# Ordering a two-layer hybrid backbone's instructions by another simulated clock

## The chip, the cores and the metric

The kernel runs on one core of a Trainium2 chip. The metric is the device time of one execution in microseconds (us); lower is better. The names of the engines are short throughout: PE is TensorE's matmul, PEld its weight load, DVE is VectorE, ACT is ScalarE, POOL is GpSimd, SP is SyncE, whose queue issues every DMA of this kernel (SPq in the profile).

## The reference

The input is 1024 latent tokens and 256 context tokens, 1024 wide, in float32, batch 1. Two layers follow, each with a modulated RMSNorm, one input projection, two branches side by side, one output projection, a gate and a residual:

- layer 0: an RWKV-7 recurrence over 8 heads of 64, in both directions, beside a Mamba-2 state-space pass over 16 heads of 64 with state 128, in chunks of 128 tokens, in both directions;
- layer 1: an mLSTM with 4 heads of 256, in chunks of 128, in both directions, beside grouped-query attention of 16 query heads on 4 key heads of 64 with a two-axis rotary embedding, over latent and context keys.

In short form:

```python
for l in range(2):
    h  = rmsnorm(x, g[l]) * (1 + scale) + shift          # the same for ctx
    y  = (rwkv || mamba)(h @ ab_w_in) if l == 0 else (mlstm || attention)(h @ cd_w_in)
    x  = x + gate * (y @ w_out)                           # ctx too, after layer 0
out = rmsnorm(x, norm_final)
```

The recurrences of the latent tokens start from the states that the context tokens left.

## The kernel before

Everything is written in one program of a tile framework: Python functions write instructions for named engines on named tiles, and when the context closes a scheduler orders them. The scheduler runs a simulation of the core: whenever an engine (or a DMA queue) is free on the simulated clock, it is given the earliest written instruction for it whose operands are there and whose buffer is free on that clock. The result is one fixed queue for each engine, which the chip runs strictly in order; waits between engines are semaphores. Each `pool.tile(..., tag=..., bufs=n)` is one of n buffers under a tag, so a load into a tag waits until an older tile of that tag has had its last reader. All loads and stores (`load`, line 179, and `store`, line 182) go through SP's one queue. All plain matmuls are recorded by line 212 and all transposes by line 215, so they are told apart by the tiles they write.

The written order is itself interleaved by hand: generators stand for streams of work, and `lockstep`, `pace` and `mix(a, b, r)` take steps of one and of another in a set ratio. The stages, in order:

1. The modulation vectors of layer 0 (`ada_mod`), and the normed input (`norm_in`), kept on chip as a high and a low part (`hh`, `hl`).
2. `l0_gemm`: the projections of layer 0, one block of 128 columns at a time. `wsplit` loads a weight block `wr`, ACT copies its high part `wh` (line 358), POOL subtracts to get the low part `wl` (line 359); PE adds three products (`hh` by `wh`, `hl` by `wh`, `hh` by `wl`) into PSUM tiles tagged `mm`. Results go to DRAM.
3. `mamba_bwd` beside the gate projections, then `mamba_fwd` beside the RWKV projections. For each chunk and group (20 steps) the forward pass loads a 1 MB broadcast tile `R` (one buffer), DVE adds to it (lines 1083 and 1084) and takes a minimum into `E` (line 1086), ACT exponentiates, POOL makes `sel` out of eight small instructions (line 1073), DVE multiplies `E` by `sel` (line 1097) and by `cb` (line 1098), PE multiplies `E` into PSUM tiles `mb`; lines 1139, 1140, 1151 and 1153 scale and add up the output, which is normed (lines 1158 to 1163) and transposed in the next step. For this stage alone PE's queue is kept as written: `with s.tc.manual_schedule(engines={mybir.EngineType.PE})`.
4. The RWKV stage: `out_part` (the Mamba half of the output projection, tiles `oa`) beside two streams in lockstep, each with two of the four pairs of heads. A stream is 20 units per pair: `rwkv_prep` (which has the square root of line 628 and the reciprocal of line 629), `rwkv_unit` (which makes the products `KB`, lines 718 and 719, and inverts a triangular matrix by doubling, tiles `rec`, `Tm`, `Xs`, `TT`) and `rwkv_chain` (the recurrence proper, tiles `ch`).
5. `out_gemm`: the rest of layer 0's output projection, and layer 1's norm.
6. `l1_gemm`: layer 1's projections beside the mLSTM, backward and forward.
7. `out_part` again, for the mLSTM half, beside the attention's keys (`attn_keys`: load `akx`, norm and rotate, split into `akk`, transpose into `tp`).
8. `attention`: scores, softmax, transposes and values, three heads deep.
9. `out_gemm` for the last half (weights loaded into `owr`, four buffers; activations into `oyr`, cast to `oyh`) and the final norm.

The scheduler's clock is chosen where the context is opened, in `kernel`:

## Time and profile before

| what | us |
|---|---|
| median of 3 runs | 3853.24 |
| lowest and highest | 3848.49, 3854.36 |
| the profiled execution | 3854.14 |
| its span, from the first to the last instruction | 3852.0 |
| PE busy in it | 3472.1 |
| DVE busy | 2324.0 |
| ACT busy | 1575.6 |
| POOL busy | 1059.2 |

The profile is one execution. An engine's busy time counts its own work and not the waits; matmuls are pipelined and their ends are modelled, so that a busy PE may still not be at its peak. Idle time of an engine is put down to the instruction whose semaphore came last. The granted clock is the share of TensorE's full speed that it had.

### The profile page before, as it was taken

What the parts mean: (1) busy time and instruction counts of PE and PEld (TensorE: products, weight loads), DVE (VectorE), ACT (ScalarE), POOL (GpSimd) and SP (SyncE); (2) the same over time, 40 slices, a digit from 0 to 9 for tenths busy, and PEclk for the clock granted to TensorE, in tenths of its full rate; (3) what the DMA queues carried; (4) which work ended last, traced back from release to release, by engine and by line L of the source; (5) the groups of instructions that cost most, each with busy time, mean ns of one, the idle gap of its engine ahead of it and who ended that gap; (6) DMA issues with size and microseconds to landing.
All of it is one profiled execution on the core that took longest, in us unless ns stands there. A gap on an engine that the chain in (4) does not pass through costs nothing.

```text
span 3852.0 us, 74955 instructions
## 1 busy us (share of the span) xinstructions
PE 3472.1 (90%) x29178; PEld 2714.9 (70%) x29178; DVE 2324.0 (60%) x4501; ACT 1575.6 (41%) x3675; POOL 1059.2 (27%) x1029
## 2 busy tenths in 40 slices
PE   7999998886898898799678999999999779999978
PEld 3687876664577777688567897788888556666547
DVE  3576487773566766667567507433343687877655
ACT  3232233333435656556433313222222226666641
POOL 0112266553322121211103112112212353333330
PEclk9999998896799988799789999999999889999999
DMA  6526454435433222211132323644543540100023
GB/s 233 178 74 196 136 176 153 158 116 177 146 120 99 66 69 68 80 50 45 47 130 82 126 82 115 199 153 148 163 156 116 184 133 17 28 22 17 15 77 112
DMA packets 394282, 429.68 MB, mean 112 GB/s; under 512 B 81376, under 2 KB 317760, under 8 KB 391368
## 3 DMA queue, kind: packets, MB, share of 16 engines
q1 hardware_dynamic: 393928, 424.90, 35.0%
q8 instruction: 230, 3.77, 0.4%
q14 instruction: 124, 1.02, 0.1%
HBM read 306.69 MB, written 118.05 MB: 110 GB/s over the span
## 4 chain that ended last, share of the span: by engine, by line
PE 48%; DVE 12%; issue 6%; DMA 6%; ACT 3%; POOL 3%; SPq 2%; ACTq 0%; DVEq 0%; POOLq 0%
PE mm L212 20%; PE rec L212 7%; PE pv L212 5%; PE tp L215 4%; PE sc L212 4%; PE lm L212 2%; PE oa L212 2%; PE ch L212 2%; SPq L179 2%; DMA lRW<-lrow 1%; DVE KB L718 1%; POOL wl L359 1%; DMA lkt<-xo 1%; DMA y<-yt 1%; DVE KB L719 1%
## 5 line engine op out<-in xcount | busy, mean ns | idle before, releaser
L212 PE MATMUL mm<-hh,wh 128*128 128x512 f32 (+1 forms) x1640 | 635.0, 387 | 0.0
L212 PE MATMUL mm<-hh,wl 128*128 128x512 f32 (+1 forms) x1640 | 610.8, 372 | 0.9 <-POOL wl L359 0.9
L212 PE MATMUL mm<-hl,wh 128*128 128x512 f32 (+1 forms) x1640 | 611.3, 373 | 0.0
L359 POOL TENSOR_TENSOR wl<-wr,wh 128x1024 fp32r<-128x1024 f32 x99 | 249.4, 2523 | 544.1 <-ACT wh L358 497.6
L212 PEld LDWEIGHTS mm<-hh,wh 128*128 128x128 f32 x1640 | 315.7, 192 | 67.8 <-issue 12.7
L212 PEld LDWEIGHTS mm<-hl,wh 128*128 128x128 f32 x1640 | 314.9, 192 | 61.4 <-issue 10.6
L212 PEld LDWEIGHTS mm<-hh,wl 128*128 128x128 f32 x1640 | 314.5, 192 | 59.4 <-issue 3.4
L1766 DVE TENSOR_REDUCE amx<-sc 128x1 f32<-128x512 f32 (+1 forms) x384 | 227.9, 596 | 85.3 <-PE sc L212 83.4
L1781 POOL TENSOR_SCALAR aP<-aP,adn,one 128x1280 f32<-128x1280 f32 x128 | 180.3, 1409 | 338.9 <-PE tp L215 116.0
L212 PE MATMUL sc<-akT,aqs 128*128 128x512 f32 (+1 forms) x768 | 247.1, 406 | 8.8 <-ACT aP L1772 8.5
L1772 ACT ACTIVATE aP<-sc,amx 128x512 f32<-128x512 f32 (+1 forms) x384 | 232.5, 618 | 40.8 <-DVE amx L1770 40.1
L212 PE MATMUL pv<-aPT,aV 128*64 128x256 f32 x1280 | 225.5, 398 | 0.5 <-DVE aG L1804 0.5
L215 PE MATMUL tp<-mk,aP 128*128 128x128 f32 x1280 | 216.2, 282 | 0.8 <-POOL aP L1781 0.8
L212 PE MATMUL mm<-wh,hh 128*128 128x256 f32 x736 | 216.4, 294 | 0.0
L212 PE MATMUL mm<-wl,hh 128*128 128x256 f32 x736 | 208.3, 283 | 3.5 <-POOL wl L359 2.6
L212 PE MATMUL mm<-wh,hl 128*128 128x256 f32 x736 | 207.8, 282 | 0.0
L215 PEld LDWEIGHTS tp<-mk,aP 128*128 128x128 f32 x1280 | 148.5, 141 | 83.2 <-issue 41.6
L1787 ACT COPY aPT<-tp 128x512 f32<-128x512 f32 (+1 forms) x256 | 121.5, 482 | 165.8 <-PE tp L215 161.3
L358 ACT CAST wh<-wr 128x1024 fp32r<-128x1024 f32 x99 | 103.2, 1045 | 150.2 <-PE mm L212 119.9
L779 ACT COPY TT<-rec 64x256 f32<-64x256 f32 x400 | 146.4, 366 | 37.8 <-PE rec L212 19.8
L212 PEld LDWEIGHTS sc<-akT,aqs 128*128 128x128 f32 x768 | 119.8, 193 | 50.9 <-ACT aP L1772 39.6
L212 PE MATMUL rec<-Tm,MT 128*64 128x64 f32 x3200 | 138.7, 230 | 13.3 <-DVE Tm L763 6.0
(417 smaller groups left out, 8035.9 us busy)
## 6 DMA issues: line engine op xcount, KB each, us to landing
wr<-in_wcd SPq DMA_DIRECT2D x60, 512.0 KB, 5.5
adaw<-in_ada SPq DMA_DIRECT2D x48, 512.0 KB, 5.2
R<-rowd SPq DMA_DIRECT2D x20, 1024.0 KB, 5.3
wr<-in_wab SPq DMA_DIRECT2D x38, 512.0 KB, 4.1
yr<-y SPq DMA_DIRECT2D x36, 512.0 KB, 4.1
xt<-xtok SPq DMA_DIRECT2D x20, 512.0 KB, 4.9
SV<-vtd SPq DMA_DIRECT2D x320, 32.0 KB, 2.1
lva<-lv SPq DMA_DIRECT2D x19, 514.0 KB, 4.3
```

The lines of the kernel that those rows point to most:

```text
L179: return s.nc.sync.dma_start(out, in_)
L212: return s.nc.tensor.matmul(out, lhsT, rhs, start=start, stop=stop)
L215: return s.nc.tensor.transpose(out, in_, ident)
L358: nc.scalar.copy(hi, raw)
L359: nc.gpsimd.tensor_sub(lo, raw, hi.bitcast(F32))
L718: nc.vector.tensor_mul(KB[H[h], :, h], P[H[h]], a[H[h]])
L719: nc.vector.tensor_mul(KB[H[h], :, 1 - h], P[H[h]], kd[H[h]])
L779: nc.scalar.copy(TT[H[h], :, H[h]], pt[H[h]])
L1766: nc.vector.tensor_reduce(mx[:, i:i + 1], ps[:, :n], AX.X, ALU.max)
L1772: nc.scalar.activation(P[:, k0:k0 + n], pss[i][:, :n], AF.Exp, bias=mx[:, 3:4], scale=0.125, accum_out=dn[:, i:i + 1])
L1781: nc.gpsimd.tensor_scalar(P, P, dn, s.one, ALU.mult, ALU.mult)
L1787: (nc.vector.tensor_copy if s0 == 0 else nc.scalar.copy)(o, pp[:, :n])
```

## The change

One argument where the context is opened. It replaces the machine that the scheduler's simulation runs on, a default model of the core, by a second one, a timeline simulation, with prices and queues of its own. The written program, its tiles, its buffers, the hand-written interleaving and the hand-kept queue of PE in stage 3 are the same.

```diff
--- before.py
+++ after.py
@@ -2021,7 +2021,7 @@
         arrays["in_" + name] = a
         aps[name] = nc.dram_tensor("in_" + name, a.shape, F32, kind="ExternalInput").ap()
     out = nc.dram_tensor("out_0", (T, D), F32, kind="ExternalOutput").ap()
-    with tile.TileContext(nc) as tc:
+    with tile.TileContext(nc, schedule_with_timeline_sim=True) as tc:
         program(nc, tc, aps, out)
     r = run_bass_kernel_spmd(nc, [arrays], core_ids=[0])
     return np.asarray(r.results[0]["out_0"]).reshape(1, T, D)
```

## The prediction

> **What bounds the kernel now.** I read three views in this order: the busy shares, the busy time by stage, and the waits of TensorE (PE) within the stages that are not full.
>
> ```profile
> span 3852.0 us, 74955 instructions
> PE 3472.1 (90%) x29178; PEld 2714.9 (70%) x29178; DVE 2324.0 (60%) x4501; ACT 1575.6 (41%) x3675; POOL 1059.2 (27%) x1029
> ```
>
> PE is busy for 90% of the span. 3852.0 - 3472.1 = 379.9 us are left in which it is not, and only there, and in the lower clock that follows a pause, can another order of the same instructions act. The stretches below are cut at the stages of the program; columns are the stretch, its length, busy us (and count) of each engine, granted clock, DMA share and GB/s.
>
> ```profile
> 100.00:500.00 400.00, 390.88 (x2005) 302.23 (x2004) 239.43 (x243) 118.29 (x191) 94.09 (x111) 1.00 0.47 151
> 500.00:860.00 360.00, 318.06 (x1531) 250.42 (x1530) 282.44 (x360) 120.35 (x181) 218.34 (x218) 0.91 0.44 147
> 860.00:1110.00 250.00, 197.49 (x1252) 131.68 (x1251) 120.76 (x192) 102.85 (x189) 75.91 (x81) 0.77 0.52 156
> 1110.00:1900.00 790.00, 698.03 (x14004) 593.40 (x14002) 535.27 (x1205) 456.67 (x1289) 158.13 (x190) 0.91 0.24 67
> 1900.00:2020.00 120.00, 80.93 (x360) 61.42 (x357) 68.96 (x135) 41.80 (x77) 5.44 (x14) 0.78 0.37 123
> 2020.00:3005.00 985.00, 944.96 (x5381) 825.78 (x5380) 423.73 (x692) 279.24 (x564) 207.40 (x163) 0.98 0.42 133
> 3005.00:3160.00 155.00, 114.34 (x493) 90.20 (x491) 124.51 (x269) 37.84 (x55) 76.25 (x83) 0.85 0.56 176
> 3160.00:3727.00 567.00, 557.45 (x3390) 345.99 (x3390) 429.99 (x1178) 359.02 (x1033) 207.26 (x155) 0.99 0.08 22
> 3727.00:3852.00 125.00, 94.38 (x424) 76.22 (x424) 61.37 (x141) 22.85 (x29) 7.81 (x3) 0.89 0.41 137
> ```
>
> Three stages, the first layer's projections (100 to 500), the second layer's projections with the mLSTM (2020 to 3005) and the attention (3160 to 3727), together 1952 us, run PE at 96 to 98% and the clock at 0.98 to 1.00: no order can give much there, though a bad one can take. The open places are the Mamba forward pass beside the RWKV projections (500 to 860: 41.9 us without PE), the start of the RWKV stage (860 to 1110: 52.5), the RWKV recurrence (1110 to 1900: 92.0), and the joints at 1900, 3005 and 3727 (39.1, 40.7 and 30.6).
>
> **The change part by part.** No instruction, tile or buffer is added or taken away. The scheduler walks a simulated clock; an engine that is free on that clock is given the earliest written instruction whose operands and buffers are ready on it. Only the clock is another. So two instructions that are ready at the same time on either clock keep the written order, and a pair changes places only where the two clocks disagree on which was ready first. PE itself cannot change between the last projections and the end of the Mamba pass, because that part fixes PE's order by hand; there the change acts through VectorE (DVE), ScalarE (ACT), GpSimd (POOL) and the DMA queue of SyncE (SP). The cost of the edit in instructions is 0 us; what follows prices the reordering place by place, against the profiled execution's 3854.14 us (its span is 3852.0; the median of the runs is 3853.24, 0.9 us less, so no correction is needed).
>
> Place 1, the Mamba pass. One stall shows what a wrong clock costs. The columns are start, length, engine, instruction, and in brackets the idle time before it.
>
> ```profile
> 587.07 9.75 POOL L1073 TENSOR_SCALAR sel<-mk,mdfd,mdt 128x128 f32<-128x128 f32 x8
> 596.79 2.82 POOL L359 TENSOR_TENSOR wl<-wr,wh 128x1024 fp32r<-128x1024 f32 x1
> 593.47 1.21 DVE L1086 TENSOR_TENSOR E<-R 128x1024 f32<-128x1024 f32 x1
> 599.64 0.33 SPq L179 DMA_DIRECT2D wr<-in_wab  x1
> 602.07 0.40 SPq L179 DMA_DIRECT2D R<-rowd  x1
> 609.88 1.23 DVE L1083 TENSOR_TENSOR R<-R,mAE 128x1024 f32<-128x1024 f32 x1 [9.18 <-DMA R<-rowd]
> 611.02 0.68 DVE L1139 TENSOR_TENSOR y<-mb,mex 128x512 f32<-128x512 f32 x1
> 611.76 1.12 PE L215 MATMUL mb<-mk,yo 128*128 128x128 f32 x4 [11.51 <-DVE y L1139]
> ```
>
> The buffer R is free at 594.7 (593.47 + 1.21), but its load is issued at 602.07, because the weight load ahead of it in SP's queue waits until POOL's split ends at 599.61 (596.79 + 2.82), and POOL came to that split late, behind eight sel instructions of 9.75 us. Then DVE holds the written-earlier L1139 behind L1083, which waits for R, and PE loses 11.51 us. Both placements say that the present clock believed POOL and this load to be earlier than they were. A clock that prices them nearer to the truth would put R ahead of the weight load, 602.07 - 594.7 = 7.4 us sooner, and L1139 ahead of L1083. PE's waits of the stage that DVE ends:
>
> ```profile
> PE mb L215 <- DVE y L1139: 16.2, 5, 11.5
> PE mb L212 <- DVE yt L1107: 4.7, 2, 2.7
> PE mb L212 <- DVE ss L1159: 4.3, 2, 2.5
> PE mb L212 <- DVE y L1139: 3.9, 2, 3.6
> ```
>
> They add to 29.1 us. Bounds: all of it (-29) if the new clock is right throughout, +42 (the stage's present idle time once more) if it is wrong elsewhere. I take half of the first, -15, since POOL's lateness is partly of a kind that no fixed price holds.
>
> That kind shows in one row: the usual time of L1097 is 1.2 us and the longest 3.4.
>
> ```profile
> L1097 DVE TENSOR_TENSOR E<-E,sel x20: 1211/1222/3419, 341.6 to 828.2; 128x1024 f32<-128x1024 f32 x20
> ```
>
> The long one starts at 597.28, 0.5 us after POOL's split, and ends at 600.70, 1.1 us after that split ends: about its own usual length behind it. The Trainium skill's page "SBUF — State Buffer", section "Summary: rules for kernel authors", says that a DVE instruction with two SBUF inputs and a GpSimd instruction that reads SBUF exclude each other, the second waiting until the first is done; the row agrees with that. By it the end of such a pair depends on which of them comes first by a fraction of a us, and a planned order keeps only part of its worth; without it the same sum would take the whole 29 us. My halving rests on the row alone.
>
> Place 2, the joint before the last projection.
>
> ```profile
> 3727.34 6.29 SPq L182 DMA_DIRECT2D y<-aG  x4
> 3734.86 8.99 SPq L179 DMA_DIRECT2D owr<-in_wcdo  x5
> 3744.38 0.42 SPq L179 DMA_DIRECT2D oyr<-y  x1
> 3752.43 1.22 PE L212 MATMUL mm<-oh,oyh 128*128 128x512 f32 x2 [20.52 <-ACT oyh L1239]
> ```
>
> PE waits 20.52 us. The load of the activations, oyr, stands behind five weight loads of which the fifth waits for one of four buffers; the stores it needs are issued by 3733.6. Issued after the fourth weight load it would be up to 8 us sooner. But the weights that it meets are also on the way, and it depends on those stores, whose landing the clock may place late again. Bounds -8 and 0; I take -4.
>
> Place 3, the joint before the attention.
>
> ```profile
> 3007.76 5.23 SPq L179 DMA_DIRECT2D aV<-av  x10
> 3013.03 0.43 SPq L179 DMA_DIRECT2D akx<-ak  x1
> 3025.05 1.97 PE L215 MATMUL tp<-mk,akk 128*128 128x128 f32 x8 [19.55 <-ACT akk L1724]
> ```
>
> Ten loads of V, needed only in the attention proper, stand ahead of the keys, and PE waits 19.55 us. All eleven are ready at once and are written in this order, so by the rule above either clock leaves them. 0, bounds -5 (the ten go behind) and +5.
>
> Place 4, the recurrence. It is a chain of short steps, and its largest wait of PE is for KB:
>
> ```profile
> PE rec L212 <- DVE KB L719: 17.1, 16, 3.1
> 1307.40 0.42 DVE L718 TENSOR_TENSOR KB<-P,a 64x256 f32<-64x256 f32 x1
> 1307.85 1.75 DVE L629 RECIPROCAL al<-al 128x256 f32<-128x256 f32 x1
> 1309.63 0.42 DVE L719 TENSOR_TENSOR KB<-P,kd 64x256 f32<-64x256 f32 x1
> 1310.11 2.07 PE L212 MATMUL rec<-AR,KB 64*128 64x128 f32 x8 [0.33 <-DVE KB L719]
> L629 DVE RECIPROCAL al<-al x20: 1732/1753/1755, 890.8 to 1545.6; 128x256 f32<-128x256 f32 x20
> ```
>
> A reciprocal of the preparation, 1.75 us, sits between the two KB products of a unit. There are 20 of them: moved to better gaps they give at most 20 x 1.75 = 35 us, and as much is lost if later-written work is let in at 20 more such places. Both ends are open and nothing in the trace leans to one of them: 0, bounds -35 and +35. The start of the stage (860 to 1110) and the joint at 1900 I leave at 0 too: the first lacks weights that are loaded only when the Mamba pass releases its space, the second is a serial finish.
>
> Sum: -15 - 4 + 0 + 0 = -19; 3854.14 - 19 = 3835 us.
>
> **The rivals.**
>
> Slower: the recurrence takes in too much. On the new clock a chain step counts as not yet ready at a moment where on the chip it is, and the free engine starts a longer, later-written piece. For it speaks that this happens already (the reciprocal above) and that the stage is the longest that is not full. Against it: most PE waits there are short. Place: 1110 to 1900. Price: one reciprocal's length in each of 40 pairs of units (80 units, two streams side by side; 790 us / 40 = 19.8 us a pair) is 40 x 1.75 = 70; half of the pairs, 35. With the 19 still won elsewhere the time is 3854 + 35 - 19 = 3870, and without it 3889; with every pair hit, 3924. It decides from 19 / 40 = 0.5 us a pair on.
>
> Slower by table loads: the order on ACT can place more changes between functions.
>
> ```profile
> L628 ACT ACT_TABLE_LOAD x20 | 25.7, 1283 | 0.4
> 591.74 1.28 ACT L1160 ACT_TABLE_LOAD   x1
> 593.03 0.20 ACT L1160 ACTIVATE ss<-ss 128x1 f32<-128x1 f32 x1
> ```
>
> All 20 square roots of the preparation have a load already, so there is little room for more; 20 more on the chain would be 20 x 1.283 = 26 us, less the 19: 3861. The Trainium skill's page "ScalarE: Activation LUTs", section "What ACT_TABLE_LOAD costs", counts a further drain of about 1.38 us to each switch; here the function starts 1.29 us after its load does, so the trace does not show it. By the page the same 20 would cost about 53 us, as an estimate.
>
> No change: where the clocks agree the queues stay, the stall at 599 does too, and the time is 3854 give or take 0.2%; the program being left wholly as it was is part of this case. For it speaks that PE's waits are short nearly everywhere, so the present clock cannot be far off.
>
> **How the numbers follow.** Forecast 0.48; slower by the recurrence 0.28; by table loads 0.08; no change 0.16. 0.2% (7.7 us) is about what a measurement of this kernel can tell from no change. The forecast's own range is 3800 (the whole 29 in place 1, 8 in place 2 and half of place 4's 35: -54) to 3846. Whole range 3785 (a little beyond, since several stages can gain at once) to 3910 (between the slower case at half and at every pair). Faster 0.48, same 0.16, slower 0.36.
>
> **What would show it.** Right: in the stretch 500 to 860 POOL's and DVE's order changed, R's load ahead of the weight load, the wait of DVE's L1083 for R (9.18 us here) gone and PE's 41.9 us without work down to about 27. At the last joint oyr is issued before the fifth weight load and 20.52 is down by about 4. The ten loads of V still lead the keys. The full stages keep their lengths (400, 985 and 567 us) within some us. Wrong: if the recurrence's 790 us grow or shrink by more than 19, they and not place 1 decide; if a full stage becomes longer, the new clock has spoiled what was hidden, a case I give no own price.

## The result, and the profile after

The kernel after takes 3892.72 us (median of 4 runs, 3890.01 to 3899.08) against 3850.86 us for the kernel before in the same comparison: ratio 1.0115, 95% interval 1.0092 to 1.0139. It is 42 us slower; 3835 was forecast. Of all executions reported below one stands apart, one of the 11 of the kernel before with the DMA queue's order in five rounds: it took 4775.22 us at a granted clock of 0.64 where the others had 0.93, and its ratio leaves it out.

The page of the profiled execution of the kernel after, its head and its busy shares:

```profile
span 3890.6 us, 74961 instructions
PE 3452.3 (89%) x29178; PEld 2756.2 (71%) x29178; DVE 2324.4 (60%) x4501; ACT 1574.1 (40%) x3671; POOL 1068.7 (27%) x1029
```

The work is the same: the same matmuls, and DVE's busy time differs by 0.4 us. PE is busy for 20 us less and idle for 58 us more. Busy time by stretch, kernel after; the last three stretches are cut where its own attention begins and ends:

```profile
100.00:500.00 400.00, 383.61 (x2000) 310.74 (x1999) 246.19 (x245) 116.82 (x186) 99.70 (x114) 0.98 0.42 136
500.00:860.00 360.00, 310.87 (x1531) 245.40 (x1530) 279.16 (x358) 120.71 (x183) 216.67 (x214) 0.93 0.43 148
860.00:1110.00 250.00, 187.90 (x939) 129.92 (x940) 119.15 (x167) 91.66 (x156) 83.30 (x79) 0.79 0.54 161
1110.00:1900.00 790.00, 701.55 (x14295) 610.86 (x14295) 534.75 (x1231) 466.56 (x1321) 156.82 (x192) 0.90 0.23 65
1900.00:2020.00 120.00, 80.52 (x366) 60.84 (x364) 66.72 (x126) 39.34 (x74) 5.64 (x15) 0.78 0.35 112
2020.00:3005.00 985.00, 946.49 (x5386) 831.58 (x5387) 429.06 (x701) 282.54 (x569) 212.92 (x163) 0.97 0.43 134
3005.00:3150.00 145.00, 107.30 (x486) 86.22 (x485) 118.43 (x249) 36.80 (x55) 65.56 (x78) 0.88 0.59 188
3150.00:3773.00 623.00, 564.58 (x3440) 373.67 (x3438) 436.16 (x1199) 359.23 (x1034) 214.43 (x159) 0.96 0.08 20
3773.00:3890.00 117.00, 90.49 (x384) 73.90 (x384) 59.93 (x140) 22.85 (x29) 7.72 (x3) 0.89 0.43 145
```

One row stands out, the attention: a stretch that PE filled now has 58 us without PE (623.00 - 564.58). Since stretches cut at fixed times mix stages, I measured each part between the same two instructions in both traces (first or last matmul of a kind):

| part, from and to | before | after | difference |
|---|---|---|---|
| start, to the first `mb` from `xt` and `E` | 462.6 | 455.3 | -7.3 |
| Mamba forward pass, to the last `mb` from `yo` | 402.4 | 410.5 | +8.1 |
| RWKV stage, to the last `ch` | 1038.2 | 1041.6 | +3.4 |
| to the last `lm` of the mLSTM | 1074.3 | 1070.6 | -3.7 |
| joint, to the first score product | 178.5 | 171.4 | -7.1 |
| attention, to the last value product | 575.9 | 623.4 | +47.5 |
| last projection, to the end | 120.1 | 117.8 | -2.3 |

They sum to +38.6, the difference of the spans. The attention alone loses more than the whole. Everything ahead of it is 6.6 us faster together in these two traces, but that cannot be told from noise: four kernels of the experiments that keep the kernel before's order up to the attention reach its first score product at 3138.0 to 3162.5 us (3156.0 here), and ten that keep the kernel after's at 3145.5 to 3159.3 (3149.4 here). Two parts repeat: the attention (576.1 to 576.4 in the two further traces that leave the old one as it is, 625.3 in the one that leaves the new one) and the Mamba pass (399.3 to 401.5 in those four, 409.8 to 411.4 in those ten). Between the attention's two ends PE is busy for 565.6 us before and 565.2 after, so by the profile its whole loss is time in which PE waits.

What PE waits for within the attention, kernel after; the columns are total us, times, longest:

```profile
PE sc L212 <- ACT aP L1772: 17.0, 31, 1.5
PE tp L215 <- ACT aPT L1787: 12.1, 19, 0.7
PE tp L215 <- POOL aP L1781: 7.0, 6, 2.6
```

The window is 3190 to 3730; in the kernel before the same view of 3190 to 3727 lists no wait of PE at all. They are many small waits, and they come in bunches. One bunch, as a timeline of the kernel after (start, length, engine, line, operation, in brackets the idle time ahead of it):

```profile
3297.35 0.15 DVE L1774 TENSOR_REDUCE adn<-adn 128x1 f32<-128x3 f32 x1
3298.04 0.54 SPq L179 DMA_DIRECT2D aqx<-aq  x1
3299.90 0.15 DVE L1775 RECIPROCAL adn<-adn 128x1 f32<-128x1 f32 x1
3302.95 0.74 POOL L1706 TENSOR_TENSOR nsw<-aqx,tab 128x256 f32<-128x256 f32 x1 [9.61 <-DVE amx L1769]
3303.68 2.37 POOL L1781 TENSOR_SCALAR aP<-aP,adn,one 128x1280 f32<-128x1280 f32 x1
3306.11 1.97 PE L215 MATMUL tp<-mk,aP 128*128 128x128 f32 x8 [2.59 <-POOL aP L1781]
```

The probabilities `aP` of a turn can be scaled from 3300.05 on, when the reciprocal is done. But POOL's queue holds a rope product `nsw` ahead of the scaling, and POOL stands idle for 9.61 us before it. (The norm of a block's queries is written one block ahead of its use, but both clocks start it far earlier: this is the sixth `nsw`, for block 5, while PE is in block 1.) The trace names a DVE step as releaser, of a tile that `nsw` does not read; the load of `aqx`, which `nsw` does read, was issued only at 3298.04. Its last packet in the trace ends at 3302.5, and `nsw` starts at 3302.95. For three other such products the trace names the load itself (total us, times, longest; 3153 to 3730):

```profile
POOL nsw L1706 <- DMA aqx<-aq: 19.2, 3, 8.6
```

The scaling starts at 3303.68 and PE's transposes at 3306.11. In the kernel before, `nsw` starts 10.0 us after the issue of its `aqx` for each of the last four blocks (3290.64 to 3300.65, 3360.30 to 3370.29, ...), and the packets of these loads end within 4 us: the load has long landed. In the kernel after it starts 3.8 to 4.9 us after the issue, so POOL is there first. DVE's order has a part in it: `nsw` has one buffer, whose last reader is the sum `nsq` (line 1708) of the block before. In the kernel before that sum starts 10.0 us behind the product of line 1707 that frees `aqx` for its load, and `nsw` starts right behind it (3289.35, 3299.35 and 3300.65); in the kernel after the two follow each other (3295.81 and 3298.02), and the buffer is free ahead of the load. The time of a bunch can be read from the same 35 us of the kernel after:

```profile
3290.00:3325.00 35.00, 29.38 (x158) 19.01 (x158) 24.69 (x66) 16.31 (x47) 12.93 (x11) 0.85 0.11 30
```

PE is idle for 5.6 us of it and its clock falls to 0.85; in the kernel before PE is busy for 34.94 of the same 35 us, at 1.00.

The attention has 8 blocks of 16 turns (96 score products each), and in blocks 0 to 6 the program writes the norm of the next block's queries (`normrope` in `attn_q`). From the starts of the 768 score products: a block from 1 to 6 takes 69.6 us before and 75.7 after; block 0 takes 75.0 and 87.3; block 7 takes 67.8 and **64.7**. As the norm runs early, its last step stands in block 5 in both traces (line 1739 at 3558.3 and 3600.8): block 6 has only PE's transposes of queries and their copies, and takes 70.2 and 68.3. Where there is no norm the new order is not slower. Yet POOL's wait for `aqx` is not all: the last `nsw` of the kernel after starts at 3462.9, in block 3, and blocks 4 and 5, with other steps of the norm, still take 76.4 and 74.4 us (69.6 and 68.8 before).

### The profile page after: what moved, and what is told of

It is laid out like the page before. It is cut to its first block, busy times and chain, and to the rows that moved or that the text cites. A ratio compares the mean times of both kernels' runs of the same rounds, so it can differ in the third digit from the quotient of the medians.

```text
span 3890.6 us, 74961 instructions
## 1 busy us (share of the span) xinstructions
PE 3452.3 (89%) x29178; PEld 2756.2 (71%) x29178; DVE 2324.4 (60%) x4501; ACT 1574.1 (40%) x3671; POOL 1068.7 (27%) x1029
## 5 line engine op out<-in xcount | busy, mean ns | idle before, releaser
L212 PE MATMUL sc<-akT,aqs 128*128 128x512 f32 (+1 forms) x768 | 228.5, 407 | 30.2 <-ACT aP L1772 29.6
L215 PE MATMUL tp<-mk,aP 128*128 128x128 f32 x1280 | 202.3, 285 | 28.0 <-ACT aPT L1787 12.3
L212 PE MATMUL pv<-aPT,aV 128*64 128x256 f32 x1280 | 195.3, 390 | 0.0
```

The source lines that it names most:

```text
L212: return s.nc.tensor.matmul(out, lhsT, rhs, start=start, stop=stop)
L215: return s.nc.tensor.transpose(out, in_, ident)
```

## The experiments

Three things were open: which queue's order costs, whether the norm is where it costs, and where the gain that the prediction placed in the Mamba pass went. "Attention" is always first score product to last value product; "block" is the mean of blocks 1 to 6.

**PE alone.** In the kernel after, PE's order in the attention is kept as written:

```diff
-        run(s.attention())
+        with s.tc.manual_schedule(engines={mybir.EngineType.PE}):
+            run(s.attention())
```

> The changed kernel, with PE's queue kept as written in the attention alone (every other queue, and every other stage, on the timeline clock). The attention, from the first score matmul to the last value matmul, is 575.9 us before the change and 623.4 after it, +47.5 of the +38.6 of the span. Theory P (PE's own order in the attention is the whole loss): the attention goes back to 576 +- 6 and the time to about 3893 - 47 = 3846. Rival Q (the order on DVE, ACT and POOL makes the loss): it stays above 610 and the time above 3880.

Measured: 3876.23 us (median of 10 runs), ratio to before 1.0052 (1.0035 to 1.0069); attention 603.4. Neither expectation came: of 47.5 us PE's written order gives back 20.

The same lines with `engines` DVE, ACT and POOL, and PE left to the clock:

> The changed kernel, with the queues of DVE, ACT and POOL kept as written in the attention alone, PE's queue there on the timeline clock. Theory P (PE's order makes the loss): the attention stays at 615 or more. Rival Q (the other engines' order makes it): it comes back to about 576 to 590.

Measured: 4076.16 us, attention 811.5. The written order of these engines is far worse than either clock's, so this says nothing of the loss; it shows that the scheduler's reordering of them is worth some 190 us here (811.5 - 623.4).

PE as written, in the kernel before:

> The kernel before the change, with PE's queue kept as written in the attention. Theory P says that the written order and the default clock's order are equally good, since the latter strays little from it (1064 switches between scores, transposes and values, against 1069 as written and 641 after the change): attention 576 +- 4, time within 0.3% of before. Rival: departing from the written order is a gain in itself when it is small, and the attention becomes longer by 5 us or more.

Measured: 3848.68 us (10 runs), ratio 0.9989 (0.9976 to 1.0003); attention 573.7. The old clock's own order of PE is worth nothing against the written one.

For the next ones, the order that one program gave an engine's instructions in the attention is forced on the other program by ordering edges between neighbours in the queue, without any wait:

```diff
+        n0 = len(s.nc.cur_bb.bb.instructions)
         run(s.attention())
+        force_order(s.tc, s.nc, n0, ORDER)
...
+        q = [i for i in mine if i.engine == getattr(mybir.EngineType, engine)]
+        for a, b in zip(o, o[1:]):
+            tc.add_manual_dep(q[b], q[a].name, info, reason="order")
```

The kernel before with PE's order of the kernel after:

> The kernel before the change, with one part of the change alone: PE's 2800 attention matmuls in the order that they have after the change, all other queues and stages on the default clock. Theory P: the attention becomes 615 to 630 and the time about 3851 + 45 = 3896, the others' order following PE's. Rival Q: the attention stays below 590.

Measured: 3889.16 us, attention 610.4, block 74.0. PE's new order, forced, costs 34.5 us. With the 27.5 left after undoing it (603.4 - 575.9) the two make 62, more than the 47.5 there are: they do not add. One reason is that the scheduler still plans the queues that are not forced, around the forced one: in this kernel DVE's order is no longer that of the kernel before either. So such a figure is the price of one queue's order together with what the others make of it.

**The other queues.** The kernel after with orders of the kernel before, in four steps:

> The kernel after, with PE's order in the attention taken from the kernel before; the orders of DVE, ACT and POOL are still planned by the new clock. Length of the attention (first score to last value product): 575.9 us before, 623.4 after, 603.4 with PE as written. Theory 'all queues together': about 603 (597 to 610), since PE as written and PE of before are nearly the same order, and the rest of the loss lies in the other engines' orders. Rival 'PE's order is the cause, and the written order was only a poor substitute for the one of before': 574 to 582.

> The kernel after with the orders of PE and DVE in the attention from the kernel before (POOL's order comes out as before's with them); only ACT and the DMA queue keep the new clock's order. If DVE's order holds the rest of the loss (27.5 us): 576 (571 to 582). If ACT's holds it: about 603. If it takes both: between, 585 to 597.

> The kernel after with the orders of PE and ACT in the attention from the kernel before; DVE and POOL keep the new clock's order. If ACT's order holds the rest of the loss: 576 (571 to 582). If DVE's holds it: about 603. If it takes both: between, 585 to 597.

> The kernel after with the orders of PE, DVE, ACT and POOL in the attention from the kernel before; only the DMA queue is still the new clock's. Theory 'the order of the queues in the attention is the whole loss': attention 576 (571 to 582), whole 3845 (3838 to 3852), so 0.995 to 1.000 of the time before. Rival 'something carried in from earlier, or the DMA queue, costs too': attention 590 or more, whole 3859 or more.

| orders taken from before | whole, us | attention | from its 33rd score product on |
|---|---|---|---|
| none (kernel after) | 3892.72 | 623.4 | 593.0 |
| PE | 3889.87 | 610.8 | 581.3 |
| PE, ACT | 3891.82 | 614.9 | 581.6 |
| PE, DVE (POOL comes out the same) | 3860.53 | 588.6 | 555.0 |
| PE, DVE, ACT, POOL | 3860.78 | 585.6 | 552.4 |
| kernel before | 3850.86 | 575.9 | 550.7 |

The first row is a median of 4 executions, the fifth of 10, the last of 4; the others are one execution each. ACT's order has no part in it. DVE's, which brings POOL's with it, has 26 us (581.3 - 555.0). The last kernel is still 9.7 us longer than before in the attention, ratio 1.0026 (1.0007 to 1.0045), which I had not expected; but 8.0 of these lie ahead of the 33rd score product, where orders made for another entry meet this program's joint. From there on it differs by 1.7 us out of 42.3. So the orders of PE, DVE and POOL together are the loss. PE's waits with PE's order alone restored (its lines are 22 higher), 3190 to 3730:

```profile
PE sc L234 <- ACT aP L1794: 12.2, 13, 2.1
PE tp L237 <- POOL aP L1803: 7.3, 10, 1.5
```

and with DVE's and POOL's restored too (26 higher):

```profile
PE tp L241 <- DVE aPT L1813: 4.6, 9, 0.5
PE tp L241 <- ACT aPT L1813: 0.4, 1, 0.4
PE sc L238 <- ACT aP L1798: 0.2, 1, 0.2
```

The waits for POOL's scaling and for the softmax behind it are gone.

**POOL alone, and the norm.** Is POOL's wait for `aqx` the cause? Its order of before in the kernel after; its order of after in the kernel before; and, in the kernel after, POOL as written (the `manual_schedule` lines with `Pool`), where the norm stands long after its load:

> The kernel after with POOL's order alone in the attention taken from the kernel before; the new clock plans PE, DVE and ACT around it. In the kernel after, POOL stands up to 9.6 us before the rope products nsw of the next block's queries (L1706) and holds the scaling of aP (L1781) behind them, and a block of 16 turns takes 75.7 us against 69.6. Theory 'POOL is held behind a load that the new clock thinks landed': block at most 71.5 us, attention 580 to 595. Rival 'the early DVE and PE pieces of the norm cost by themselves': block 73 to 76 us, attention 605 to 625.

> The kernel before with POOL's order alone in the attention taken from the kernel after; the old clock plans the rest around it. Theory 'POOL is held behind a load': POOL waits for the load of aqx before L1706, block of 16 turns 72 to 76 us (69.6 in the kernel before), attention 590 to 615. Rival: block 69.6 to 70.5, attention 576 to 581, since the load is issued as in the kernel before and has landed.

> The kernel after with POOL's instructions in the attention kept in the written order: the norm of the next block's queries is then written 6 turns into a block, long after its load. Theory 'POOL is held behind a load': the waits of L1706 for aqx are gone, block at most 71.5 us, attention 575 to 595. Rival 'the norm costs wherever it stands': block 73 or more, attention 600 to 625.

Measured, one execution each: 3877.16, 3884.37 and 3885.65 us; attention 606.3, 600.3 and 615.8; block 73.3, 72.8 and 76.9. POOL's idle time before `nsw` from 3190 to 3730 in the second of them, the kernel before with the new order (lines 21 higher):

```profile
L1727 POOL TENSOR_TENSOR nsw<-aqx,tab x19: 718/725/734, 3189.7 to 3463.4; 128x256 f32<-128x256 f32 x19
  DVE adn L1795: 38.0, 4
```

Against 5.0 us before; each of the four starts 4.6 us after the issue of its load. So the wait came along with POOL's order, and 24 us with it (600.3 - 575.9), again with DVE and ACT planned anew around it. But taking POOL's order out of the kernel after gives only 17 of 47.5 us, and as written, with no idle time before `nsw` left, the block is longer still. "POOL is held behind a load" is one part, and as the cause of the whole it falls.

The norm itself taken out, in both kernels: blocks 1 to 7 use block 0's queries. This leaves out all of `attn_q` for seven blocks, so also the load, the split into two parts and 112 of PE's 128 transposes of queries.

```diff
-                    qg = [s.attn_q(b + 1)]
+                    s.qst[b + 1] = s.qst[0]
```

> The kernel before with the norm of the queries left out for blocks 1 to 7 of the attention (they use block 0's queries). It fixes what the attention takes under the old clock without those pieces. In block 7, which has no next norm to make, 96 score products take 67.8 us: attention 8 x 67.8 = 542 (532 to 550).

> The kernel after with the norm of the queries left out for blocks 1 to 7 of the attention. Theory 'the new clock loses only where norm pieces stand among the softmax steps': block 7 takes 64.7 us there, so 8 x 64.7 = 518, and with the same edges 515 to 540, not longer than the kernel before without the norm. Rival 'the new order is worse in the softmax chain itself': 10 us or more above the kernel before without the norm.

First and last start of the value products and of the score products, kernel before without the norm, then kernel after without it:

```profile
L212 PE MATMUL pv<-aPT,aV x1280: 379/379/431, 3156.8 to 3695.6; 128*64 128x256 f32 x183
L212 PE MATMUL sc<-akT,aqs x768: 276/397/793, 3138.0 to 3680.3; 128*128 128x512 f32 x128, 128*128 128x256 f32 x64
```

```profile
L212 PE MATMUL pv<-aPT,aV x1280: 378/380/431, 3162.8 to 3705.3; 128*64 128x256 f32 x183
L212 PE MATMUL sc<-akT,aqs x768: 274/392/796, 3145.5 to 3692.6; 128*128 128x512 f32 x128, 128*128 128x256 f32 x64
```

Attention 557.9 and 560.2 us, block 68.6 and 68.8; whole 3818.47 and 3823.91 (one execution each). Both are longer than I had expected (I had left out the 13 to 16 us from the last score product to the last value product, and the 64.7 us of the kernel after's block 7 are no measure of a steady block), but the comparison is clear: without `attn_q` the two orders differ by 2.3 us, with it by 47.5. Its pieces cost 18 us under the old clock (575.9 - 557.9) and 63 under the new (623.4 - 560.2). Blocks 6 and 7 above say which of them: with the transposes and without the norm the new order was not slower.

**The Mamba pass.** The prediction had put its gain there, and the pass is 8 us longer. DVE's order of before in the kernel after, by the same edges:

```diff
         with s.tc.manual_schedule(engines={mybir.EngineType.PE}):
+            n0 = len(s.nc.cur_bb.bb.instructions)
             mix(g, s.mamba_fwd(), s.mix2)
+            force_order(s.tc, s.nc, n0, ORDER)
```

> The kernel after with DVE's order in the Mamba forward pass taken from the kernel before (PE's is fixed by hand in both). Length of the pass (first to last mb product): 402.4 us before, 410.5 after. Theory 'the earlier load of R gains, and DVE's new order of the ss and yo steps eats it': pass 385 to 400. Rival 'the load of R was not what set the pass': 402 to 411. If the two orders only fit each their own clock: more than 411.

Measured, one execution: pass 418.8 us, whole 3899.27. DVE's new order is not what takes the gain back; the old one, among the other new orders, is worse. Then the reverse: only the DMA queue's new order, in the kernel before.

> The kernel before with the order of the DMA queue SP in the Mamba forward pass taken from the kernel after, so R's load stands ahead of the weight load as the prediction wanted it; DVE, ACT and POOL are planned by the old clock around it. Length of the pass: 402.4 us before, 410.5 after. If the prediction's step was right (15 us lie in that load): 381 to 395. Rival 'the load was one of several waits that follow each other, and the next one takes its place': 398 to 407.

Measured, one execution: pass 386.1 us, **16.3 shorter** than in the trace of the kernel before (13 to 15 shorter than in the four traces that share its order), whole 3833.83. The stall of the prediction, in this kernel (lines 21 higher), from the timeline of SP's queue:

```profile
577.17 0.32 SPq L200 DMA_DIRECT2D R<-rowd  x1
587.99 1.75 SPq L203 DMA_DIRECT2D y<-yt  x4
598.90 0.33 SPq L200 DMA_DIRECT2D wr<-in_wab  x1
```

The load of `R` that stood behind this weight load now stands ahead of it. Counted from the first matmul of the pass it is issued at 119 instead of 139 us. PE's queue is the same in both, so its lead can be read step by step from the transposes of `yo`: it is level with the kernel before up to the step ahead of the stall (0.6 us behind), 10.8 us ahead right behind it and 15.8 at the end. The stretch of the pass in the view of busy times, and the wait of PE that held the stall:

```profile
458.50:844.60 386.10, 348.99 (x1735) 276.22 (x1733) 323.21 (x400) 143.08 (x214) 264.39 (x244) 0.95 0.44 153
```

```profile
PE mb L236 <- DVE y L1160: 8.5, 5, 5.2
```

PE is idle for 37 us of it (45.6 in the kernel before, at a clock of 0.92), and the wait of `mb` for `y` that was 16.2 us with a longest of 11.5 is 8.5 with a longest of 5.2. In the kernel after, that load of `R` is early too (130 us into the pass), DVE's wait for `R` is down and PE's for `y` of line 1139 nearly gone, but others are new: by the same transposes PE is 14.6 us behind the kernel before ahead of the stall, 5.8 behind it, and 8.1 at the end. The kernel after, first DVE's idle time ahead of its work on `R`, then PE's waits, over the pass:

```profile
  DMA R<-rowd: 6.8, 4
```

```profile
PE mb L215 <- DVE yo L1163: 26.4, 8, 8.5
PE mb L212 <- DVE y L1151: 22.1, 8, 4.9
PE mb L215 <- DVE y L1139: 2.4, 1, 2.4
```

PE now waits 48.5 us for the norm and the sums at the end of a step (`yo`, and `y` at line 1151), which took 3.3 us and nothing in the kernel with the DMA queue's order alone. Which of DVE's, ACT's and POOL's new orders does it was not separated.

**A version that beats both.** The kernel after with the attention's orders from the kernel before with PE as written, a first tenth of each queue left free (`o = o[FREE[engine]:]` ahead of the edges):

> An attempt at a version that beats both. The kernel after, with the orders of PE, DVE, ACT and POOL in the attention from the kernel before with PE as written, except for the first tenth of each queue, which the new clock orders itself, so that the entry of the attention fits what stands before it. All before the attention is 6.5 us ahead in the kernel after, the attention took 573.7 us with those orders, 2.2 under the kernel before: 3853 - 6.5 - 2.2 = 3844 (3838 to 3853), ratio 0.996 to 1.000. If the entry jams as it did with the orders of before (8 us): 3852.

Measured: 3852.62 us (11 runs), ratio 1.0003 (0.9994 to 1.0012). The entry jams again (the first 32 score products take 30.5 us against 25.2); from there on the attention takes 551.2 against 550.7. The 6.5 us ahead of the attention that were counted on are not there to be had either, as the spread of that part above shows. The other way, the kernel before with the one queue's order that gained, in five rounds, alone and with PE as written in the attention:

> The kernel before with the DMA queue's order of the kernel after in the Mamba forward pass, once more and against the kernel before in five rounds. One look gave 3833.8, with the pass 16.3 us shorter: ratio 0.9945 to 0.9975 (3834, 3829 to 3841) if that holds; 0.998 to 1.000 if the one look was a lucky one.

> The same, and PE kept as written in the attention, which gave 573.7 us against 575.9 in the kernel before. If the two add: 3832 (3825 to 3838), 2 us below the kernel with the DMA queue's order alone; if the order of PE in the attention is worth nothing: equal to it within 2 us.

Measured: 3839.52 us (11 runs), ratio **0.9964** (0.9951 to 0.9976), and 3835.64 us (8 runs), 0.9961 (0.9947 to 0.9974), against 3851.21 for the kernel before. The passes are 386.8 and 386.3 us. By the first ratio the order of 237 DMA issues is worth 14 us (9 to 19 by its interval); PE's order in the attention adds nothing that can be told.

## Why the prediction was wrong, step by step

- **The full stages.** This is the step that failed: "the full stages keep their lengths", and the attention entered the sum at 0 because PE was at 98% there, with "no order can give much there, though a bad one can take" and "a case I give no own price". The first half held: no order tried made the attention more than 2.2 us shorter. The second half was the result: +47.5 us. The other two full stages did keep their lengths (the part that holds the first is 7.3 us shorter, the one with the mLSTM 3.7), so being full is not the reason by itself. What sets the attention apart could have been read from the profile: DVE 430 and ACT 359 busy us of 567, in short steps of a chain that PE waits on, with the norm's pieces among them. The measured time lies within the whole range of 3785 to 3910, but by luck: no term of that range stood for this loss.
- **Place 1, -15.** The mechanism was right and the size too, for the DMA queue: with its order alone the pass is 386.1 to 386.8 us in three profiles, against 402.4 in the kernel before and 399.3 to 401.5 in four more with its order, so 12 to 16 us shorter, and 11.4 of 16.3 come at the stall that was shown. What was wrong is that this would be the net effect of the new clock on the pass. It also changed the other queues, and PE's waits for `yo` and `y` (48.5 us) took the gain and 8 us more: in the stretch 500 to 860 PE's 41.9 us without work went to 49.1 and not to 27. The bounds of -29 and +42 held it.
- **Place 2, -4.** Right: `oyr` is issued ahead of the fifth weight load and PE's wait falls from 20.52 to 17.55, 3.0 us. From SP's queue and PE's, kernel after:

```profile
3775.74 2.12 SPq L179 DMA_DIRECT2D owr<-in_wcdo  x4
3778.49 0.45 SPq L179 DMA_DIRECT2D oyr<-y  x1
3784.37 0.33 SPq L179 DMA_DIRECT2D owr<-in_wcdo  x1
3790.35 1.22 PE L212 MATMUL mm<-oh,oyh 128*128 128x512 f32 x2 [17.55 <-ACT oyh L1239]
```

- **Place 3, 0.** Right: the ten loads of V (one of them at 3005.84) still lead the keys, and the wait is 20.55 against 19.55.

```profile
3007.79 4.24 SPq L179 DMA_DIRECT2D aV<-av  x9
3012.07 0.43 SPq L179 DMA_DIRECT2D akx<-ak  x1
3026.59 1.97 PE L215 MATMUL tp<-mk,akk 128*128 128x128 f32 x8 [20.55 <-ACT akk L1724]
```

- **Place 4 and the start of the stage, 0.** About right as far as it can be told: +3.4 us for the whole RWKV stage, whose length differs by 13 us between traces of one order (1031.8 to 1045.0 with the old). The reciprocal did leave its gap: PE's wait for the second `KB` falls from 17.1 to 1.0 us. But the wait for `Xs`, a little further on in the same unit, rises from 8.3 to 17.6, and the one for `MN` from 3.0 to 9.5. Kernel after, 1110 to 1900:

```profile
PE rec L212 <- DVE Xs L769: 17.6, 18, 2.8
PE rec L215 <- DVE MN L730: 9.5, 8, 3.9
PE rec L212 <- DVE KB L719: 1.0, 1, 1.0
```

- **The rivals.** The recurrence needed 19 us to decide and had 3.4; that its price without the 19, 3889, lies near the measured 3892.72 is chance. Table loads did not grow (ACT has 3671 instructions instead of 3675, and the square roots still load 20 times).

- **The rule that two instructions ready on both clocks keep the written order** told place 3, where DMA loads that are ready together follow each other. It says nothing of the case that decided: a later-written piece (the norm of a later block) that is let in ahead of an earlier-written one.

What stays open: why the new clock lets the norm's pieces in where it does. For POOL it is shown that `nsw` is queued so that it starts at the landing of its load instead of 6 us later, behind a DVE sum that now comes early; that the clock believed the load to be earlier is argued from it. For PE's and DVE's order the trace gives no single place that costs: PE's old order gives back 12.6 us by itself (623.4 - 610.8), DVE's and POOL's on top of it another 22 (610.8 - 588.6), and which of DVE's moves does it was not separated.

## What to carry to other kernels

A stage in which the bounding engine is at 96 to 98% is not safe from a new order: of three such stages here one lost 47.5 us and two nothing. Price it by the engines that must keep up, not by the idle time that is left. When a scheduler's clock is changed, look at where late-needed work (a later block's preparation) stands in the in-order queues of the helping engines, and at whether its loads have landed by then. Take over an order queue by queue and stage by stage: here one queue's order in one stage gained 14 us and the whole lost 42.

## What the runs showed of the hardware

Two instructions of different engines that hold each other up were clearer than expected. In the kernel before, the subtraction of line 1739 on DVE (two operands) starts 0.37 us after POOL's scaling of 1.41 us has begun, and takes 2.11 us; it ends 1.07 us after POOL does, nearly its own length. In the kernel after with POOL as written, DVE is first by 0.27 us: DVE takes 1.20 us and POOL's scaling 2.21. The two rows of the kernel before, then the two of the other:

```profile
3349.22 1.41 POOL L1781 TENSOR_SCALAR aP<-aP,adn,one 128x1280 f32<-128x1280 f32 x1 [3.00 <-DVE amx L1770]
3349.59 2.11 DVE L1739 TENSOR_TENSOR aqq<-nsq,aqq 128x1024 fp32r<-128x1024 f32 x1
```

```profile
3342.76 1.20 DVE L1739 TENSOR_TENSOR aqq<-nsq,aqq 128x1024 fp32r<-128x1024 f32 x1
3343.03 2.21 POOL L1781 TENSOR_SCALAR aP<-aP,adn,one 128x1280 f32<-128x1280 f32 x1 [3.41 <-DVE adn L1775]
```

So in both pairs whichever comes second pays. The Trainium skill's page "SBUF — State Buffer", section "Summary: rules for kernel authors", says of a DVE instruction with two SBUF inputs and a GpSimd one that reads SBUF that the second to issue blocks until the first finishes. The two pairs agree with it. The norm is made of such two-operand pieces on DVE; how much of the 47.5 us comes from this was not measured, but little can: between the two ends of the attention DVE is busy for 2.2 us and POOL for 5.6 us more than before (436.4 against 434.3, 214.4 against 208.8).

The second is the clock. In the bunch of waits above, with PE idle for 5.6 of 35 us, the granted clock is 0.85 in the stretch, and in the whole attention 0.96 against 0.99; yet PE's busy time there stayed the same to 0.4 us. That is no rule: for the same products it is 541.0 us in the kernel after with POOL's old order and 575.1 in the kernel before with POOL's new one, and the reason is open. What the lower clock costs is not shown.
